# Raw weights one pair ahead, stores and reloads some steps behind their work, and reloads from ACT's queue, in two units of half products

## The chip, the cores and the metric

The kernel runs on one core of a Trainium2 chip. The engines of a core work side by side and wait for each other through semaphores: TensorE (PE in the profile), VectorE (DVE), ScalarE (ACT) and GpSimd (POOL) compute; each of them, and SyncE (SP), has a queue of its own that it works off in order. A transfer is issued from one of these queues: an instruction `sy.dma_start` stands in SP's queue, `ac.dma_start` in ACT's. It may wait there for its data or its buffer, and what stands behind it waits too. The metric is the device time of one execution in microseconds (us); lower is better.

## The reference

What is computed is one step of a layer of a streaming encoder: from the residual stream `x` (1,152 rows: 1,024 of a prompt and 8 x 16 of running streams; width 1,024) an input projection, two token mixers side by side (a state-space branch of width 2,048 and an attention branch of width 1,024), and then, cut to what the change touches:

```python
y = layer_norm(DN_ALPHA * x
               + (sigmoid(g_m) * (y_m @ w_br_m) + sigmoid(g_a) * (y_a @ w_br_a)) @ w_out)
```

`y_m` is 1,152 x 2,048, `y_a` 1,152 x 1,024, and each branch matrix projects to 1,024 columns. All of it is float32. The kernel holds every factor as two parts, `hi` (rounded) and `lo` (the rest), and makes a product of three matmuls: hi by hi, lo by hi, hi by lo.

## The kernel before

Up to about 1667 us of the profile the kernel computes the input projection, both mixers and the first half of `y_a @ w_br_a` (the quarter A0). The change touches what comes after, in four stages that PE works through in this order.

**Unit 0** (1667 to 1795 us) and **unit 1** (1850 to 1950 us) each compute one half of `y_m @ w_br_m` by half products in the manner of Winograd and Strassen: sums of blocks of rows (S1 to S4, D1, D2 and the plain blocks A11, A12, A22) by blocks of weights and their sums. Unit 0 takes rows 4 to 11 of the sixteen 128-row tiles of `y_m`, unit 1 the other eight. A unit (`unit`) has 4 pairs `p` of output columns; a pair has 8 pieces of weights, the plain blocks B11, B21, B12, B22 and the sums T1, T2, T4, T3, and takes 11 products. A product (`product`) is 12 matmuls of 128x128 by 128x384: three each over four steps k. After a pair's product its result is added into `acc` (DVE, L1485 and L1491) or copied there (ACT, L1483).

A piece is made three pieces ahead of its products by `prepare`. It has a tile `pc` in a ring of four (the tags `wh` and `wl`, two each): the sum of raw weights (L1423; on POOL in the first pair, else on DVE), the cast to the hi part on ACT (L1457), the lo part on POOL (L1458). The raw weights are `wu` (B11 and B21, one tile, loaded at L1411) and `wv` (B12 and B22, L1416); `load_pair` asks SP for the next pair's as soon as `prepare` has used this pair's. In the profile `u01d` is the fourth part of a name: unit 0, pair 1, accumulator d1 or d2; `u02m` is one of the m's of pair 2.

The sums T of unit 1 are made early, during unit 0, by the generator `sums_of_weights`: raw weights `we` to the tags `yr` (a ring of four) by SP at L1432, then for each of the four T's a sum on DVE (L1423), a cast on ACT (L1439), a lo part on DVE (L1440) into a tile `te`, and a store to `t_d` in memory by SP (L1441). Unit 1's `prepare` then only loads such a piece back (`pc<-t_d`, SP, L1454). The generator is worked off by `flow.tick()`, called twice in a product: `yield 3` lets three ticks pass before the next part is written into the queues. The order in which the units' instructions stand in each queue is the order in which this code writes them (`manual_schedule`); outside the units a planner with a cost model sets it.

After the sums, the same generator (`rows_c01`) loads the second half of the rows of `y_a` (`yr1`, L1587, and `yc1`, L1588) and makes them hi and lo (`part`, L1596 and L1597) for **quarter A1** (1795 to 1850 us, tile `dq`): the second half of `y_a @ w_br_a`, 288 matmuls, whose weights are `wr92` and the next (`fetch` L214, cast `wh` L226, lo part `wl` L227 on POOL). At the end of unit 0 (piece B22 of its last pair) stand `rows_c2` (the last third of those rows) and `first_rows(1)`, which loads the first two row tiles of unit 1 (`send`, L1338 and L1341) and scales them on DVE (`scaled`, L1345). The rest of unit 1's rows is loaded and summed during A1 by `load_sums` (hi parts L1329, lo parts L1330).

In unit 1 `seconds` fetches both halves of `y_a @ w_br_a` (`pa`, `pb`; L1640 and L1641) and the gate (L1642), adds them and multiplies (DVE, L1644 and L1646); `final` and `finish` load the other branch's gate (`gm`, L1654), multiply (DVE, L1662) and add (POOL, L1663). In this unit one product of each pair is copied by ACT to a tile `sh` (L1520).

**The out projection** (1950 to 2057 us, tile `out`) multiplies the merged rows U (`uhi` and `ulo`, made by `parts_of_u` on ACT L1689 and DVE L1690) with `w_out` (L1777 to L1779). The last third of the columns of `acc` is merged during it by `late` (L1676 to L1679, from tiles `lt`). A block of 128 rows that is done is normalized on DVE (L1807 to L1815) and stored.

Of the kernel before, what the change touches and what calls it, by code (L numbers as in the profile page):

```python
# [149 lines left out]
def trunk_step(ctx: ExitStack, tc: tile.TileContext, I, O):  # L150
# [1196 lines left out]
    def first_rows(v):  # L1347

        kts = ROWS[v]
        rb = [None]  # L1350
        pair_ = [send(kts[0], rb, *(() if v else (lazy["f0"], "gs"))), send(kts[1], rb)]
        for i in range(2):
            scaled(kts[i], pair_[i], rb)
        return pair_

    def load_sums(v, pair_=None):
# [5 lines left out]
        rb = [None]  # L1362
        pair_ = pair_ or first_rows(v)
        for i in range(4):
            y0, y1 = pair_
            if i:
                scaled(kts[2 * i], y0, rb)
                scaled(kts[2 * i + 1], y1, rb)
# [57 lines left out]
    def sums_of_weights():  # L1426

        early = {}
        for p in range(4, 8):
# [4 lines left out]
            if p == 4:  # L1434
                yield 4
            for i, n in enumerate(SUMS):
                x = sum_of(early, p, n, ve)
# [3 lines left out]
                sy.dma_start(t_d[4 * (p - 4) + i], o[:].bitcast(F32))  # L1441
                yield 3

    pieces = []

    def prepare():
# [6 lines left out]
        if p >= 4 and name in SUMS:  # L1453
            sy.dma_start(t[:].bitcast(F32), t_d[4 * (p - 4) + SUMS.index(name)])  # L1454
# [5 lines left out]
        if p % 4 < 3:  # L1460
            if name == ("T4" if p < 4 else "B21"):
                load_pair(p + 1, 0)
            if name == ("T3" if p < 4 else "B22"):
                load_pair(p + 1, 1)
# [112 lines left out]
    A1, ys = [], []  # L1577

    def rows_c01():
# [4 lines left out]
        for i in range(4):  # L1584
            y = mp.tile([P, T], F32, tag="yr", name=f"yr1{i}", bufs=4)[:, 0:2 * CW]
            ys.append(mp.tile([P, CW], F32, tag=("gt", "s4")[i % 2], name=f"yc1{i}", bufs=2)[:])
            sy.dma_start(y, ya_d[4 + i][:, 0:2 * CW])  # L1587
            sy.dma_start(ys[i], ya_d[4 + i][:, ch(2)])  # L1588
            yield 3
            for c in range(2):  # L1590
                part(c, i, y[:, ch(c)])
            yield 3
# [6 lines left out]
    def rows_c2():  # L1599

        A1.append(tuple(ap.tile([P, 4, CW], F32R, tag=f"a{x}2", name=f"ya1{x}2") for x in ("hi", "lo")))
        for i in range(4):
            part(2, i, ys[i])

    def steps_0(p, piece):

        if p == 3 and piece == "B22":
            flow.drain()
            rows_c2()
            lazy["rows"] = first_rows(1)  # L1610
# [23 lines left out]
    def seconds(*ps):  # L1634

        for j in (j for p in ps for j in (2 * p, 2 * p + 1)):
# [8 lines left out]
            yield 2  # L1645
            ve.scalar_tensor_tensor(g, t, 1.0, g, ALU.add, ALU.mult)  # L1646
            yield 1
# [24 lines left out]
    def late(j):  # L1672
# [3 lines left out]
        ve.tensor_tensor(x0, x0, x1, ALU.add)  # L1676
# [31 lines left out]
    def steps_1(p, piece):  # L1708
# [9 lines left out]
        if at == 5 and 0 < p < 3:  # L1718
# [192 lines left out]
```

## Time and profile before

| | us |
|---|---|
| median of 3 runs (lowest, highest) | 2062.91 (2058.42, 2064.49) |
| the profiled execution, its own time | 2066.38 |
| its span in the trace | 2064.6 |
| unit 0: 1667.0 to 1795.0 | 128.0 |
| quarter A1: 1795.0 to 1849.7 | 54.7 |
| unit 1: 1849.7 to 1950.3 | 100.6 |
| out projection: 1950.3 to 2057.3 | 107.0 |
| tail | 7.3 |

Over the whole span PE is busy 2021.1 us (98%), DVE 1355.0 (66%), ACT 951.5 (46%) and POOL 541.5 (26%). A row of the profile names a line, an engine, an operation and the tiles (out<-in), with start and duration or a count and a mean; in square brackets stands how long the engine was idle before it, and what ended that. `SPq` is SP's queue: a duration there is the time that its instructions held the queue, waiting included. A row of waits reads: who waited, for whom; us in total, times, longest us. The clock (PEclk) is the TensorE clock that was granted, as a share of full speed. A busy PE is not always PE at its own pace: the stages differ in the time that the same matmul takes.

### The profile page before, as it was taken

What the parts mean: (1) busy time and instruction counts of PE and PEld (TensorE: products, weight loads), DVE (VectorE), ACT (ScalarE), POOL (GpSimd) and SP (SyncE); (2) the same over time, 40 slices, a digit from 0 to 9 for tenths busy, and PEclk for the clock granted to TensorE, in tenths of its full rate; (3) what the DMA queues carried; (4) which work ended last, traced back from release to release, by engine and by line L of the source; (5) the groups of instructions that cost most, each with busy time, mean ns of one, the idle gap of its engine ahead of it and who ended that gap; (6) DMA issues with size and microseconds to landing.
All of it is one profiled execution on the core that took longest, in us unless ns stands there. A gap on an engine that the chain in (4) does not pass through costs nothing.

```text
span 2064.6 us, 36468 instructions
## 1 busy us (share of the span) xinstructions
PE 2021.1 (98%) x14199; PEld 1867.5 (90%) x14199; DVE 1355.0 (66%) x2237; ACT 951.5 (46%) x2059; POOL 541.5 (26%) x716
## 2 busy tenths in 40 slices
PE   9999999999999999999999999999999997899898
PEld 7899999999999999999888898898888987899886
DVE  4145666676766766633778778778677765566677
ACT  5124556456555555543555555544544543351310
POOL 0012535354544445331100100100010032313410
PEclk9999999999999999999999999999999998999998
DMA  7423232333233242425556666656657854477753
GB/s 220 162 65 99 72 125 84 123 95 123 90 117 120 78 148 67 140 95 180 174 190 214 201 184 214 194 188 206 192 181 227 281 183 163 174 239 279 263 181 107
DMA packets 139180, 332.37 MB, mean 161 GB/s; under 512 B 20360, under 2 KB 80256, under 8 KB 128768
## 3 DMA queue, kind: packets, MB, share of 16 engines
q1 hardware_dynamic: 121424, 238.75, 35.6%
q10 hardware_dynamic: 17584, 91.30, 12.9%
q8 instruction: 111, 1.82, 0.4%
q14 instruction: 61, 0.50, 0.1%
HBM read 255.66 MB, written 74.33 MB: 160 GB/s over the span
## 4 chain that ended last, share of the span: by engine, by line
PE 76%; DVE 9%; DMA 6%; issue 3%; POOL 3%; ACT 2%; SPq 0%; ACTq 0%; DVEq 0%; POOLq 0%
PE d L247 17%; PE d L249 16%; PE d L248 16%; PE s L953 3%; PE o L1028 2%; PE y L738 2%; PE v L337 2%; PE v L336 2%; PE v L335 2%; PE so L1103 1%; PE dS L679 1%; POOL pc L1458 1%; PE y L742 1%; PE ss L1081 1%; PE dq L249 1%
## 5 line engine op out<-in xcount | busy, mean ns | idle before, releaser
L247 PE MATMUL d<-xh,wh 128*128 128x384 f32 x2112 | 736.4, 349 | 0.0
L249 PE MATMUL d<-xh,wl 128*128 128x384 f32 x2112 | 708.3, 335 | 0.0
L248 PE MATMUL d<-xl,wh 128*128 128x384 f32 x2112 | 707.2, 335 | 0.0
L247 PEld LDWEIGHTS d<-xh,wh 128*128 128x128 f32 x2112 | 396.7, 188 | 19.4 <-issue 8.7
L248 PEld LDWEIGHTS d<-xl,wh 128*128 128x128 f32 x2112 | 397.2, 188 | 0.8
L249 PEld LDWEIGHTS d<-xh,wl 128*128 128x128 f32 x2112 | 396.5, 188 | 0.0
L227 POOL TENSOR_TENSOR wl<-wr,wh 128x1024 fp32r<-128x1024 f32 x37 | 89.9, 2429 | 180.2 <-ACT wh L226 168.2
L958 ACT ACTIVATE st<-s,ckt 128x256 f32<-128x256 f32 (+1 forms) x320 | 115.5, 469 | 16.5 <-PE s L953 14.2
L1018 ACT ACTIVATE st<-st 128x1024 f32<-128x1024 f32 x80 | 83.2, 1062 | 46.6 <-DVE st L1013 43.6
L962 POOL TENSOR_TENSOR st<-st,mask_bf 128x256 f32<-128x256 f32 x64 | 51.3, 822 | 192.4 <-ACT st L958 192.2
L707 ACT ACTIVATE m<-ce,nacum 128x128 f32<-128x128 f32 x288 | 96.9, 392 | 5.7 <-PE y L738 5.7
L230 DVE SCALAR_TENSOR_TENSOR wl<-wr,wh 128x1024 fp32r<-128x1024 f32 x50 | 62.1, 1243 | 34.9 <-ACT wh L229 34.8
L634 POOL TENSOR_TENSOR wx<-xdt,wdt 128x256 f32<-128x256 f32 x72 | 54.1, 753 | 85.2 <-DVE xdt L632 85.2
L1458 POOL TENSOR_TENSOR pc<-wu,pc 128x512 fp32r<-128x512 f32 x28 | 37.5, 1348 | 140.2 <-ACT pc L1457 140.2
L226 ACT CAST wh<-wr 128x1024 fp32r<-128x1024 f32 x48 | 50.3, 1049 | 51.0 <-PE d L248 44.6
L1028 PE MATMUL o<-st,vt 128*64 128x256 f32 (+1 forms) x640 | 69.4, 363 | 0.6
L1028 PEld LDWEIGHTS o<-st,vt 128*64 128x64 f32 x640 | 42.9, 136 | 27.3 <-ACT st L1018 4.0
L853 ACT ACTIVATE gate<-d,bcol 128x384 f32<-128x384 f32 x48 | 27.8, 578 | 72.2 <-PE d L249 47.1
L229 ACT ACTIVATE wh<-wr 128x1024 fp32r<-128x1024 f32 x50 | 52.7, 1054 | 14.3 <-PE d L248 10.7
L1039 DVE TENSOR_TENSOR st<-st 128x1024 f32<-128x1024 f32 (+1 forms) x40 | 57.4, 1436 | 0.8
L687 POOL TENSOR_TENSOR S<-S,ea 128x256 f32<-128x256 f32 x56 | 37.8, 675 | 75.9 <-DVE S L688 64.6
L336 PE MATMUL v<-vl,xh 128*128 128x512 f32 x144 | 56.4, 391 | 0.4 <-DVE vl L329 0.4
(929 smaller groups left out, 4372.1 us busy)
## 6 DMA issues: line engine op xcount, KB each, us to landing
wr<-in_wt SPq DMA_DIRECT2D x88, 512.0 KB
kc<-in_cache_k ACTq DMA_DIRECT2D x32, 1024.0 KB
vc<-in_cache_v ACTq DMA_DIRECT2D x32, 1024.0 KB
ce<-ac_d SPq DMA_DIRECT2D x96, 192.0 KB
sb<-cs_d ACTq DMA_DIRECT2D x16, 576.0 KB
yr<-ym_d SPq DMA_DIRECT2D x16, 576.0 KB
gate_d<-gate SPq DMA_DIRECT2D x45, 192.0 KB
s<-in_state_ssm SPq DMA_DIRECT2D x8, 1024.0 KB
```

Source lines behind the costliest of these rows:

```text
L227: lazy.get("sub", po).tensor_tensor(lo[:, :cols], raw[:, :cols], hi[:, :cols].bitcast(F32), ALU.subtract)
L230: ve.scalar_tensor_tensor(lo[:, :cols], raw[:, :cols], scale, hi[:, :cols].bitcast(F32), ALU.mult, ALU.subtract)
L247: te.matmul(out, wh, xh, start=(k == 0), stop=False)
L248: te.matmul(out, wh, xl, start=False, stop=False)
L249: te.matmul(out, wl, xh, start=False, stop=(k == n - 1))
L336: te.matmul(d, xh, wl, start=False, stop=False)
L707: ac.activation(m[:, j, :], ce[:, j * P:(j + 1) * P], AF.Abs, bias=nacum[:, b, h:h + 1])
L953: te.matmul(ps2[:, e, 256 * x + q0:256 * x + 256], kk[hr, ks], qq[hr, qs], start=(at == 0), stop=(at == 2))
L958: ac.activation(S[j][:, e, kb, q0:], ps2[:, e, 256 * x + q0:256 * x + 256], AF.Identity, bias=ckt[:, kb, 2 * hp + e:2 * hp + e + 1])
L1018: ac.activation(w, w, AF.Exp, scale=-1.0)
L1028: te.matmul(o[64 * e:64 * e + 64, 256 * at + q0:256 * at + 256], vt[:, kb, 64 * e:64 * e + 64], S[j][:, e, kb, q0:256], start=(kb == 0), s ...
L1458: po.tensor_tensor(t[:, 512:1024], out, t[:, 0:512].bitcast(F32), ALU.subtract)
```

## The change

The change moves work and adds none to PE. `sums_of_weights` loads the raw weights of the next pair after the first sum of the pair before, and issues each store to `t_d` one step later, ahead of the next sum. The rows `yr1` and `yc1` are loaded inside it (`load_second`) and no longer after it. `load_pair` is called some pieces later than before (`coming`: one piece in unit 0, two and three in unit 1). The reloads `pc<-t_d` stand in ACT's queue. `first_rows(1)` only sends, and one product earlier; the scaling stands at the start of `load_sums`. `seconds` runs once over all eight j at an even pace of ten ticks. In `late` the first add is on POOL; the late rows and the last `parts_of_u` come at other places of the out projection; `split_wo(3)` and `load_wo(6)` come before `finish(2)`, and `rows_of_wo` begins 0, 2, 3, 1.

```diff
--- before.py
+++ after.py
@@ -1348,10 +1348,7 @@
 
         kts = ROWS[v]
         rb = [None]
-        pair_ = [send(kts[0], rb, *(() if v else (lazy["f0"], "gs"))), send(kts[1], rb)]
-        for i in range(2):
-            scaled(kts[i], pair_[i], rb)
-        return pair_
+        return [send(kts[0], rb, *(() if v else (lazy["f0"], "gs"))), send(kts[1], rb)], rb
 
     def load_sums(v, pair_=None):
 
@@ -1359,13 +1356,11 @@
         slot.update({"A11": (Xb[0], 0), "A12": (Xb[0], 4), "A22": (Xb[1], 0), "S1": (Xb[1], 4),
                      "D1": (Xb[2], 0), "D2": (Xb[2], 4)})
         kts = ROWS[v]
-        rb = [None]
-        pair_ = pair_ or first_rows(v)
+        pair_, rb = pair_ or first_rows(v)
         for i in range(4):
             y0, y1 = pair_
-            if i:
-                scaled(kts[2 * i], y0, rb)
-                scaled(kts[2 * i + 1], y1, rb)
+            scaled(kts[2 * i], y0, rb)
+            scaled(kts[2 * i + 1], y1, rb)
             if i < 3:
                 pair_ = [send(kts[2 * i + 2], rb), send(kts[2 * i + 3], rb)]
             for name, y, c in (("D1", y0, c2), ("A11", y0, c0), ("D2", y1, c2), ("A12", y1, c0), ("A22", y1, c1)):
@@ -1425,23 +1420,52 @@
 
     def sums_of_weights():
 
-        early = {}
-        for p in range(4, 8):
+        early, stores = {}, []
+
+        def load(p):
             for j, names in enumerate((("B11", "B21"), ("B12", "B22"))):
                 t = mp.tile([P, 1024], F32, tag="yr", name=f"we{p}_{j}", bufs=4)
                 sy.dma_start(t[:], weights_of(p, j))
                 early[p, names[0]], early[p, names[1]] = t[:, 0:512], t[:, 512:1024]
-            if p == 4:
-                yield 4
+
+        def store():
+            for fn in stores:
+                fn()
+            stores.clear()
+
+        load(4)
+        yield 4
+        for p in range(4, 8):
             for i, n in enumerate(SUMS):
+                store()
+                if i == 1:
+                    if p < 7:
+                        load(p + 1)
+                    else:
+                        load_second(0)
+                        load_second(1)
                 x = sum_of(early, p, n, ve)
                 o = ap.tile([P, 1024], F32R, tag=("ahi0", "alo0", "ahi1", "alo1")[i], name=f"te{p}_{i}")
                 ac.copy(o[:, 0:512], x)
                 ve.tensor_tensor(o[:, 512:1024], x, o[:, 0:512].bitcast(F32), ALU.subtract)
-                sy.dma_start(t_d[4 * (p - 4) + i], o[:].bitcast(F32))
+                stores.append(lambda o=o, i=i, p=p: sy.dma_start(t_d[4 * (p - 4) + i], o[:].bitcast(F32)))
                 yield 3
-
-    pieces = []
+        store()
+        load_second(2)
+        load_second(3)
+        yield 4
+
+    rows2 = []
+
+    def load_second(i):
+
+        y = mp.tile([P, T], F32, tag="yr", name=f"yr1{i}", bufs=4)[:, 0:2 * CW]
+        yc = mp.tile([P, CW], F32, tag=("gt", "s4")[i % 2], name=f"yc1{i}", bufs=2)[:]
+        sy.dma_start(y, ya_d[4 + i][:, 0:2 * CW])
+        sy.dma_start(yc, ya_d[4 + i][:, ch(2)])
+        rows2.append((y, yc))
+
+    pieces, coming = [], []
 
     def prepare():
 
@@ -1451,17 +1475,18 @@
         if p >= 4 and name in SUMS:
-            sy.dma_start(t[:].bitcast(F32), t_d[4 * (p - 4) + SUMS.index(name)])
+            ac.dma_start(t[:].bitcast(F32), t_d[4 * (p - 4) + SUMS.index(name)])
         else:
             out = sum_of(raw, p, name, ve if p else po) if name in SUMS else raw[p, name]
             ac.copy(t[:, 0:512], out)
             po.tensor_tensor(t[:, 512:1024], out, t[:, 0:512].bitcast(F32), ALU.subtract)
         pieces.append(t)
         if p % 4 < 3:
-            if name == ("T4" if p < 4 else "B21"):
-                load_pair(p + 1, 0)
-            if name == ("T3" if p < 4 else "B22"):
-                load_pair(p + 1, 1)
+            for which, last, gap in ((0, "T4", 1), (1, "T3", 1)) if p < 4 else ((0, "B21", 2), (1, "B22", 3)):
+                if name == last:
+                    coming.append((n + gap, p + 1, which))
+        while coming and coming[0][0] <= n:
+            load_pair(*coming.pop(0)[1:])
 
     def product(d, n, name, first, last):
 
@@ -1574,7 +1599,7 @@
-    A1, ys = [], []
+    A1 = []
 
     def rows_c01():
 
@@ -1582,14 +1607,9 @@
         for c in range(2):
             A1.append(tuple(ap.tile([P, 4, CW], F32R, tag=f"a{x}{c}", name=f"ya1{x}{c}") for x in ("hi", "lo")))
         for i in range(4):
-            y = mp.tile([P, T], F32, tag="yr", name=f"yr1{i}", bufs=4)[:, 0:2 * CW]
-            ys.append(mp.tile([P, CW], F32, tag=("gt", "s4")[i % 2], name=f"yc1{i}", bufs=2)[:])
-            sy.dma_start(y, ya_d[4 + i][:, 0:2 * CW])
-            sy.dma_start(ys[i], ya_d[4 + i][:, ch(2)])
-            yield 3
             for c in range(2):
-                part(c, i, y[:, ch(c)])
-            yield 3
+                part(c, i, rows2[i][0][:, ch(c)])
+                yield 2
 
     def part(c, i, y):
         h, l = A1[c][0][:, i, :], A1[c][1][:, i, :]
@@ -1600,14 +1620,15 @@
 
         A1.append(tuple(ap.tile([P, 4, CW], F32R, tag=f"a{x}2", name=f"ya1{x}2") for x in ("hi", "lo")))
         for i in range(4):
-            part(2, i, ys[i])
+            part(2, i, rows2[i][1])
 
     def steps_0(p, piece):
 
+        if p == 3 and piece == "B12":
+            flow.drain()
+            lazy["rows"] = first_rows(1)
         if p == 3 and piece == "B22":
-            flow.drain()
             rows_c2()
-            lazy["rows"] = first_rows(1)
 
@@ -1631,9 +1652,9 @@
 
     G, U, wraw, pending, wo = {}, {}, {}, [], {}
 
-    def seconds(*ps):
-
-        for j in (j for p in ps for j in (2 * p, 2 * p + 1)):
+    def seconds():
+
+        for j in range(8):
             G[j] = mp.tile([P, T], F32, tag="yr", name=f"pa{j}", bufs=4)
             xt = ap.tile([P, 4 * CW], F32, tag="ahi0", name=f"pb{j}")
             g, x, t = G[j][:, 0:2 * CW], xt[:, 0:2 * CW], xt[:, 2 * CW:]
@@ -1642,9 +1663,9 @@
             sy.dma_start(t, gate_d[8 + j][:, 0:2 * CW])
             yield 5
             ve.tensor_tensor(g, g, x, ALU.add)
-            yield 2
+            yield 1
             ve.scalar_tensor_tensor(g, t, 1.0, g, ALU.add, ALU.mult)
-            yield 1
+            yield 4
 
     def final(*jcs):
 
@@ -1673,7 +1694,7 @@
 
         x0, x1, ta, tm = (pending.pop(0) for _ in range(4))
         a = acc[:, j, ch(2)]
-        ve.tensor_tensor(x0, x0, x1, ALU.add)
+        po.tensor_tensor(x0, x0, x1, ALU.add)
         ve.scalar_tensor_tensor(x0, ta, 1.0, x0, ALU.add, ALU.mult)
         ve.scalar_tensor_tensor(a, tm, 1.0, a, ALU.add, ALU.mult)
         po.tensor_tensor(a, a, x0, ALU.add)
@@ -1715,8 +1736,6 @@
             if at < 2:
                 final((b - 2, at))
             finish(1)
-        if at == 5 and 0 < p < 3:
-            flow.start(seconds(p + 1))
         if p == 0 and at == 4:
             load_wo(2)
         if p == 1 and at == 4:
@@ -1739,21 +1758,21 @@
     with tc.manual_schedule():
         sums_last(1)
         todo.pop(0)
-        flow.start(seconds(0, 1))
+        flow.start(seconds())
         unit(1, steps_1)
         flow.drain()
     sums_stack.close()
     raw_stack.close()
     op = ma_stack.enter_context(tc.tile_pool(name="op", bufs=1, reuse_waits="tile"))
     wo[0] = ready.pop(0)
-    finish(2)
+    split_wo(3)
+    load_wo(6)
     split()
     wo[1] = ready.pop(0)
-    split_wo(3)
-    load_wo(6)
+    finish(2)
     parts_of_u(0, (6, 7))
     load_late(0)
-    rows_of_wo = (0, 2, 1, 3, 4, 5, 6, 7)
+    rows_of_wo = (0, 2, 3, 1, 4, 5, 6, 7)
...
@@ -1786,14 +1805,14 @@
                     split_wo(k + 4)
                 if k == 2:
                     load_wo(7)
-                if k % 2:
-                    late(k // 2)
+                if k > 2:
+                    late(k - 3)
             parts_of_u(1, range(8))
         for j in range(3):
-            if c == 1 and j < 2:
-                late(4 + 2 * j)
-                late(5 + 2 * j)
-            if c == 1 and j == 2:
+            if c == 1 and j == 0:
+                for i in (5, 6, 7):
+                    late(i)
+            if c == 1 and j == 1:
                 parts_of_u(2, range(8))
...
```

What this does to the queues shows at three places. First SP's queue in unit 0, from the raw weights of pair 4 on (`we4`; `te4_0` is its first T). Before:

```order
L1432 DMA we4_0_18288<-in_wbr 128x1024
L1432 DMA we4_1_18290<-in_wbr 128x1024
L1441 DMA t_d_80<-te4_0_18326 128x1024
L1441 DMA t_d_80<-te4_1_18351 128x1024
L1411 DMA wu1_18377<-in_wbr 128x1024
L1441 DMA t_d_80<-te4_2_18386 128x1024
L1441 DMA t_d_80<-te4_3_18411 128x1024
L1416 DMA wv1_0_18420<-in_wbr 128x512
L1416 DMA wv1_1_18422<-in_wbr 128x512
L1432 DMA we5_0_18449<-in_wbr 128x1024
L1432 DMA we5_1_18451<-in_wbr 128x1024
L1441 DMA t_d_80<-te5_0_18454 128x1024
```

and now:

```order
L1428 DMA we4_0_18288<-in_wbr 128x1024
L1428 DMA we4_1_18290<-in_wbr 128x1024
L1451 DMA t_d_80<-te4_0_18326 128x1024
L1428 DMA we5_0_18350<-in_wbr 128x1024
L1428 DMA we5_1_18352<-in_wbr 128x1024
L1451 DMA t_d_80<-te4_1_18355 128x1024
L1451 DMA t_d_80<-te4_2_18388 128x1024
L1406 DMA wu1_18421<-in_wbr 128x1024
L1411 DMA wv1_0_18441<-in_wbr 128x512
L1411 DMA wv1_1_18443<-in_wbr 128x512
L1451 DMA t_d_80<-te4_3_18413 128x1024
L1451 DMA t_d_80<-te5_0_18454 128x1024
```

The loads `we5` moved from behind four stores and `wu1`, `wv1` to behind the first store; the last store of a pair moved behind `wu1` and `wv1`.

Second ACT's queue at the end of unit 0: `pc31` is the unit's last piece, `ya1hi2` and `wh92` are what quarter A1 needs, `ym1h` are parts of unit 1's rows. Before:

```order
L1457 CAST pc31_19086<-wv3_0_18877 128x512
L1483 COPY acc_17605<-u03d2_19106 128x384
L1596 CAST ya1hi2_19146<-yc10_18839 128x384
L1596 CAST ya1hi2_19146<-yc11_18906 128x384
L1596 CAST ya1hi2_19146<-yc12_18961 128x384
L1596 CAST ya1hi2_19146<-yc13_19021 128x384
L226 CAST wh92_19164<-wr92_19104 128x1024
L1329 CAST ym1h2_19203<-yr10_19156 128x384
L1329 CAST ym1h0_19199<-yr10_19156 128x384
L1329 CAST ym1h2_19203<-yr11_19160 128x384
L1329 CAST ym1h0_19199<-yr11_19160 128x384
L1329 CAST ym1h1_19201<-yr11_19160 128x384
```

and now:

```order
L1481 CAST pc31_19086<-wv3_0_18904 128x512
L1329 CAST ym1h0_19197<-yr10_19119 128x384
L1329 CAST ym1h0_19197<-yr11_19123 128x384
L1329 CAST ym1h1_19199<-yr11_19123 128x384
L1508 COPY acc_17605<-u03d2_19106 128x384
L1329 CAST ym1h2_19201<-yr10_19119 128x384
L1329 CAST ym1h2_19201<-yr11_19123 128x384
L1329 CAST ym1h1_19199<-yr11_19123 128x384
L1616 CAST ya1hi2_19152<-yc10_18741 128x384
L1616 CAST ya1hi2_19152<-yc11_18745 128x384
L1616 CAST ya1hi2_19152<-yc12_18843 128x384
L1616 CAST ya1hi2_19152<-yc13_18847 128x384
L226 CAST wh92_19162<-wr92_19104 128x1024
```

Six casts of `ym1h` stand ahead of the four of `ya1hi2` and of `wh92`; before they stood behind.

Third ACT's queue in the first pair of unit 1 (`sh0` is that pair's shared copy, `pc36` to `pc39` its last four pieces). Before:

```order
L1520 COPY sh0_19764<-u10m1_19750 128x384
L1457 CAST pc37_19797<-wv4_0_19714 128x512
L1457 CAST pc38_19820<-wv4_1_19716 128x512
L1457 CAST pc40_19861<-wu5_19614 128x512
L1457 CAST pc41_19878<-wu5_19614 128x512
L1520 COPY sh1_19973<-u11m1_19954 128x384
```

and now:

```order
L1478 DMA pc35_19728<-t_d_80 128x1024
L1545 COPY sh0_19764<-u10m1_19750 128x384
L1478 DMA pc36_19766<-t_d_80 128x1024
L1481 CAST pc37_19797<-wv4_0_19712 128x512
L1481 CAST pc38_19815<-wv4_1_19714 128x512
L1478 DMA pc39_19838<-t_d_80 128x1024
L1481 CAST pc40_19856<-wu5_19730 128x512
L1481 CAST pc41_19873<-wu5_19730 128x512
L1478 DMA pc42_19910<-t_d_80 128x1024
L1478 DMA pc43_19935<-t_d_80 128x1024
L1545 COPY sh1_19967<-u11m1_19952 128x384
```

The reloads stand between the copies and casts; `sh0` stands ahead of `pc36`, and `sh1` behind `pc43`.

## The prediction, made before the result was known

> **What bounds the kernel now.** The change touches only what runs after 1667 us, so I read that stretch first by stage (busy time of each engine in a window; after the window's bounds stands its length, PEclk is the granted TensorE clock as a share of full speed, and after it come the DMA share and GB/s). The rows are unit 0, quarter A1, unit 1 and the out projection.
>
> ```profile
> core 0: us, PE busy (x) PEld busy (x) DVE busy (x) ACT busy (x) POOL busy (x), PEclk, DMA share, GB/s
> 1667.00:1795.00 128.00, 107.36 (x530) 101.46 (x528) 65.96 (x100) 44.47 (x91) 46.38 (x34) 0.88 0.48 174
> 1795.00:1849.70 54.70, 52.01 (x290) 51.67 (x290) 41.86 (x59) 29.92 (x61) 13.49 (x6) 0.97 0.64 207
> 1849.70:1950.30 100.60, 94.55 (x530) 93.09 (x528) 60.96 (x90) 18.04 (x33) 37.01 (x28) 0.98 0.78 271
> 1950.30:2057.30 107.00, 102.59 (x481) 85.20 (x480) 78.11 (x141) 16.90 (x32) 17.29 (x10) 0.97 0.49 165
> ```
>
> TensorE (PE) is the bound in all four stages, but not at its own pace. That pace is in the records of the quarter before, where nothing waits:
>
> ```profile
> L247 PE MATMUL dq<-ya0h,wh x96: 334/334/334, 1617.1 to 1666.5; 128*128 128x384 f32 x96
> L249 PE MATMUL dq<-ya0h,wl x96: 334/334/334, 1617.5 to 1666.9; 128*128 128x384 f32 x96
> ```
>
> Three such lines make 288 matmuls between 1617.1 and 1666.9, 49.8 us or 0.173 us each. A unit has 528 of the same shape, so 91.6 us. Unit 0 therefore loses 128.0 - 91.6 = 36.4 us, A1 (288 matmuls) 54.7 - 49.9 = 4.8, unit 1 100.6 - 91.6 = 9.0. The waits of PE from 1667 us on say what for (total, times, longest, us):
>
> ```profile
> PE u01d L1471 <- ACT pc L1457: 8.8, 2, 6.1
> PE u02m L1471 <- ACT pc L1457: 6.1, 2, 3.1
> PE u12m L1471 <- DMA pc<-t_d: 3.8, 2, 3.2
> PE dq L249 <- POOL wl L227: 2.0, 1, 2.0
> PE out L1777 <- ACT uhi L1689: 1.7, 1, 1.7
> PE u11m L1471 <- DMA pc<-t_d: 1.6, 1, 1.6
> PE out L1779 <- DVE ulo L1690: 1.1, 1, 1.1
> PE u00m L1471 <- ACT pc L1457: 1.0, 1, 1.0
> PE u00m L1473 <- POOL pc L1458: 0.7, 1, 0.7
> PE dq L247 <- ACT wh L226: 0.7, 1, 0.7
> ```
>
> In unit 0 four stalls of PE, 14.9 us, end with the cast of a piece. The cast is not slow; it is late. Inside that unit's window VectorE (DVE) and SP's queue wait thus:
>
> ```profile
> DVE we L1423 <- DMA we<-in_wbr: 23.0, 3, 8.3
> DVE te L1440 <- ACT te L1439: 14.6, 16, 2.4
> SPq L1441 <- DVE te L1440: 59.7, 13, 9.3
> ```
>
> SP issues in order, and the store of one `te` tile makes it wait for DVE. So everything behind a store is late: the next pair's `we` loads, and `wu`. These rows of SP's timeline show it (start, duration; the four stores hold the queue from 1701 to 1715, and `wu` comes after):
>
> ```profile
> 1691.27 0.90 SPq L1432 DMA_DIRECT2D we<-in_wbr  x2
> 1701.08 12.18 SPq L1441 DMA_DIRECT2D t_d<-te  x4
> 1715.59 0.33 SPq L1411 DMA_DIRECT2D wu<-in_wbr  x1
> ```
>
> A `we` load asked for at 1691.7 lands at 1698.85; the DVE stands before its sum for 8.33 us, and behind that sum in DVE's queue stands what PE needs. First the chain of waits, then the timeline:
>
> ```profile
> 1691.74 7.11 DMA we<-in_wbr
> ```
>
> ```profile
> 1698.94 0.69 DVE L1423 TENSOR_TENSOR we<-we,we 128x512 f32<-128x512 f32 x1 [8.33 <-DMA we<-in_wbr]
> 1700.89 0.69 PE L1471 MATMUL u01d<-ym0h,pc 128*128 128x384 f32 x1 [2.74 <-ACT pc L1457]
> 1703.06 0.52 PE L1472 MATMUL u01d<-ym0l,pc 128*128 128x384 f32 x1
> 1703.38 0.52 PE L1473 MATMUL u01d<-ym0h,pc 128*128 128x384 f32 x1
> ```
>
> The last two rows are the second price: after the gap the matmuls start 0.32 us apart, not 0.173, each 0.147 us late. Unit 0's idle time on PE is 128.0 - 107.36 = 20.6 us; the other 15.8 of its 36.4 are about 107 matmuls at that half pace, which is why the window's clock reads 0.88. A stall costs its gap and some 20 matmuls (3 us) behind it.
>
> **The change, part by part.** Durations (count, total, mean ns, idle before), from unit 0:
>
> ```profile
> L1458 POOL TENSOR_TENSOR pc<-wu,pc 128x512 fp32r<-128x512 f32 x18 | 23.5, 1310 | 48.5 <-ACT pc L1457 48.5
> L1440 DVE TENSOR_TENSOR te<-we,te 128x512 fp32r<-128x512 f32 x16 | 15.5, 968 | 14.6 <-ACT te L1439 14.6
> L1439 ACT CAST te<-we 128x512 fp32r<-128x512 f32 x16 | 9.9, 619 | 38.3 <-DVE we L1423 36.4 <-issue 2.0
> L1423 DVE TENSOR_TENSOR we<-we,we 128x512 f32<-128x512 f32 x8 | 8.2, 1019 | 23.0 <-DMA we<-in_wbr 23.0
> ```
>
> *Raw weights one pair ahead, stores one step behind (unit 0).* No instruction is removed. A `we` pair is now asked for behind the first store of the pair before, some three quarters of a pair (11 products of 12 matmuls, 22.9 us) ahead of its first sum, against a load of 7.11 us. That covers DVE's three load waits, 23.0 us, and with them the three largest stalls on PE. A store issued one step later finds its lo part done, so SP's 59.7 us of waiting shrink and `wu`, `wv` follow in time; each of those goes behind at most three stores, all ready. What is late next is DVE's own order. A step is sum 1.02, cast 0.62 on ACT, lo 0.97, so 2.6 us in line; in the second pair two such steps (5.2 us) stand ahead of the sum for T4, and that piece needs cast 0.62 and POOL 1.31 behind it. In the first pair the T sums are on POOL in both kernels, and nothing there changes. I leave to the four pairs 3.4 us (its two short gaps on `u00m`, 1.7, and some 11 slow matmuls, 1.6), 4.5 (between nothing and 5.2 + 3), 2.5 and 1: 11.4 together. Gain 36.4 - 11.4 = 25.0. Bounds: the three load stalls alone (11.8 us of gaps and 3 us each behind, so 20.8, less 3 for a new T4 stall) give 18; everything but 5 us gives 31. If the early loads collided with others, the cover of 17 us less 7.11 would have to go first.
>
> [...]
>
> *First rows of unit 1 scaled before the last rows of A1 (end of unit 0).* The row loads move by one product. But on ACT six casts of `ym1` now stand ahead of the four `ya1hi` casts and of `wh92`, with which A1 begins. DVE, ACT and POOL of before, each from its timeline:
>
> ```profile
> 1793.48 1.96 DVE L1597 TENSOR_TENSOR ya1lo<-yc,ya1hi 128x384 fp32r<-128x384 f32 x4
> 1795.37 4.84 DVE L1345 SCALAR_TENSOR_TENSOR yr<-yr,mcol,rsb 128x1152 f32<-128x1152 f32 x2
> ```
>
> ```profile
> 1792.94 1.75 ACT L1596 CAST ya1hi<-yc 128x384 fp32r<-128x384 f32 x4 [1.60 <-PE u03m L1473]
> 1794.60 1.04 ACT L226 CAST wh<-wr 128x1024 fp32r<-128x1024 f32 x1
> ```
>
> ```profile
> 1795.77 3.21 POOL L227 TENSOR_TENSOR wl<-wr,wh 128x1024 fp32r<-128x1024 f32 x1 [4.65 <-ACT wh L226]
> ```
>
> Before, `wh92` was done at 1795.64, 0.6 us after unit 0's end, for which PE waited 0.7, and then 2.0 for `wl`. Now six casts (2.6 us at the 0.44 of a `ya1hi` cast) and the two scalings that they wait for come first. In SP's timeline the loads are asked for 10 us ahead of the unit's end:
>
> ```profile
> 1784.98 0.43 SPq L1338 DMA_DIRECT2D yr<-ym_d  x1
> ```
>
> So the scalings are mostly under unit 0; I put `wh92` 2.4 us after the unit's end, so 1.8 more idle and some 8 slow matmuls more: 3 us lost. Bounds: 0 (all six done under the last product) and 7 (the whole 4.84 and the casts after it).
>
> *Reloads from ACT's queue, loads with a gap, `seconds` at an even pace (unit 1).* The stalls were SP's order too: `pc<-t_d` stood behind `pb`, whose buffer waited for DVE. From the chain of waits there:
>
> ```profile
> 1897.68 5.99 DMA pb<-pa_d
> ...
> 1908.54 4.87 DMA pc<-t_d
> ```
>
> From the buffer's release to its use four to five products of 2.08 us (12 x 0.173) pass, 8.3 to 10.4 us; the reload takes 4.87. On ACT the instruction waits for the same product that frees the buffer; ahead of it can stand one `sh` copy, which is ready about 1 us after that. So 2 to 4 us are spare. The sixteen issues of 0.4 us each on ACT are nothing: it is busy 18.04 of 100.6 us. The three DMA stalls (5.4 us) and their slow matmuls (about 3) go, and I leave 3 of the 9.0: gain 6, from 2 to 8.
>
> *Late rows (out projection).* The eight first adds leave DVE for POOL, which is busy 17.29 of 107.0; all `late` parts are done sooner, and the last third of U (the out projection's input) is made one column group earlier. The two stalls there (`uhi` 1.7, `ulo` 1.1) and about 2.7 us of slow matmuls behind them can go, 5.5; what is earlier makes other DVE work later in a stage where DVE is busy 78.11 of 107.0, so gain 4, from 1.5 to 5.5. `split_wo(3)` ahead of `finish(2)`: the start waits for the last product's add as before, nothing. The tail is unchanged.
>
> The sum: -25 + 3 - 6 - 4 = -32. The profiled execution took 2066.38 (span 2064.6), so 2034.4. It lies 3.5 above the median of the runs, 2062.91; against that the same 32 give **2031**.
>
> **The rivals.**
>
> *DVE's queue takes the place of the loads.* The T4 stall that I give to one pair comes in three, each as large as a before one: a 3 us gap with 3 us behind. 18 instead of the 8 left for these pairs, 10 more, and a slower A1 (2): 2043. For it speaks the 14.6 us that DVE stands for its own cast round trip, inside the queue that also carries the piece sums; against it, that DVE's 65.96 us fill only 64% of the 103 us that unit 0 would take.
>
> *Nearly all goes.* Unit 0 keeps only its first pair's 3.4 (-33), A1 0, unit 1 -8, out -5: 46 us, 2017. The 17 us of cover speak for it; the DVE order against.
>
> *Slower: reloads that share the DMA engines.* In unit 1 the reloads no longer queue behind SP's loads but run beside them, at a stage whose share is 0.78 and which would run faster still. If a reload beside another 512 KB load takes twice 4.87 us, 9.7, it passes the 8 us budget by about 1.7, plus 3 us of slow matmuls: 4.7 a piece. It decides from 8 us of transfer on; with twelve of the sixteen hit, 56 us, so 2031 + 6 + 56 = 2093, and with nine 2079. Against it: unit 1 moves 271 GB/s, 27.3 MB, which in 95 us are 287 GB/s, and the loads on SP are now spread evenly. [...]
>
> *The change doesn't do what it says:* stores one step behind still wait for lo parts, and SP's queue stays the bound with `wu` behind three stores. Then unit 0 gains only about 5, the rest stands: 2063 - 5 + 3 - 6 - 4, 2051.
>
> **How the numbers follow.** Forecast 0.50, DVE's queue 0.22, nearly all 0.13, slower 0.08, not as said 0.07. The forecast's own bounds, all best or all worst, are -44.5 and -14.5 (2018 to 2048); the range takes in the rivals on both sides but the slower one: 2015 to 2052. A measurement of this kernel tells about 0.3% (6.2 us) from no change. Faster, below 2056.7: the first three and half of the last, 0.88; within 0.3%: 0.06; slower: 0.06.
>
> **What would show it.** Unit 0 at about 103 us with DVE's waits on `we` gone and SP's on `te` small; if it stays above 115 with waits of PE on `pc` casts behind DVE, the first rival holds. A1 at 57 to 58, its first matmul 2 to 3 us after unit 0's last; a shorter A1 refutes my third step. Unit 1 at 94 to 95, no wait on `pc<-t_d`; more of these waits than three would be the reloads' rival. Out at 103, no waits for `uhi` and `ulo` in its middle. The prediction is wrong altogether if unit 0 is not the stage that changes most.

## The result, and the profile after

| | before | after |
|---|---|---|
| median, us (lowest to highest) | 2062.86 (2058.42 to 2064.49) | 2030.66 (2027.91 to 2032.09) |
| profiled execution, own time / span | 2066.38 / 2064.6 | 2031.07 / 2029.3 |
| unit 0 | 128.0 | 99.7 |
| quarter A1 | 54.7 | 55.9 |
| unit 1 | 100.6 | 96.7 |
| out projection | 107.0 | 102.9 |

The ratio is 0.9846, 95% interval 0.9827 to 0.9864: faster by 32 us. The four stages of the kernel after, in the view by windows (columns as before):

```profile
1666.80:1766.50 99.70, 95.52 (x529) 92.84 (x527) 74.02 (x101) 44.21 (x91) 47.77 (x34) 0.98 0.65 229
1766.50:1822.40 55.90, 53.05 (x288) 52.54 (x289) 39.34 (x56) 28.83 (x59) 12.72 (x6) 0.94 0.56 187
1822.40:1919.10 96.70, 93.69 (x530) 93.39 (x529) 59.75 (x89) 17.93 (x32) 37.59 (x28) 0.98 0.80 285
1919.10:2022.00 102.90, 100.64 (x482) 84.63 (x480) 74.30 (x133) 17.44 (x33) 26.54 (x19) 0.98 0.52 173
```

28.3 of the 35.3 us between the two spans come from unit 0. (The profiled execution before was 3.5 us above its median, so the spans differ by more than the medians do.) Unit 0's four stalls of 14.9 us are gone; PE's longest waits after 1667 us are now these:

```profile
PE u12m L1496 <- DMA pc<-t_d: 3.0, 1, 3.0
PE dq L247 <- ACT wh L226: 2.6, 1, 2.6
PE out L1797 <- DVE wl L230: 2.2, 1, 2.2
PE u01m L1496 <- ACT pc L1481: 1.3, 1, 1.3
PE u02m L1498 <- POOL pc L1482: 0.9, 2, 0.7
PE u01m L1498 <- POOL pc L1482: 0.7, 1, 0.7
PE u00m L1498 <- POOL pc L1482: 0.7, 1, 0.7
```

In unit 0 DVE has no wait for a `we` load any more (it was 23.0 us). The raw weights of pair 6 are asked for at 1692.84 and first used at 1704.84, with the DVE busy up to that moment. SP's queue and then DVE's, from the timeline:

```profile
1692.84 1.25 SPq L1428 DMA_DIRECT2D we<-in_wbr  x2
1695.84 8.83 SPq L1451 DMA_DIRECT2D t_d<-te  x3
```

```profile
1703.63 0.69 DVE L1450 TENSOR_TENSOR te<-we,te 128x512 fp32r<-128x512 f32 x1 [0.69 <-ACT te L1449]
1704.24 0.69 DVE L1418 TENSOR_TENSOR wu<-wu 128x512 f32<-128x512 f32 x1
1704.84 0.68 DVE L1418 TENSOR_TENSOR we<-we,we 128x512 f32<-128x512 f32 x1
```

The second row of DVE's is the sum for T4 in the second pair; it comes behind two steps of `te`, and PE waits for its piece, the one longer stall that unit 0 has left. It isn't new: the kernel before had it at the same product (1.2 us for the cast, 0.7 for the lo part). The rows of the changed kernel:

```profile
1705.69 0.44 PE L1496 MATMUL u01m<-ym0h,pc 128*128 128x384 f32 x1 [1.28 <-ACT pc L1481]
1707.05 0.48 PE L1498 MATMUL u01m<-ym0h,pc 128*128 128x384 f32 x1 [0.74 <-POOL pc L1482]
1707.64 0.52 PE L1497 MATMUL u01m<-ym0l,pc 128*128 128x384 f32 x1
```

### The profile page after: what moved, and what is told of

The parts are those of the page before. It is cut to its first block, busy times and chain, and to the rows that moved or that the text cites. A ratio compares the mean times of both kernels' runs of the same rounds, so it can differ in the third digit from the quotient of the medians.

```text
span 2029.3 us, 36477 instructions
## 1 busy us (share of the span) xinstructions
PE 2006.7 (99%) x14199; PEld 1859.9 (92%) x14199; DVE 1356.7 (67%) x2229; ACT 951.6 (47%) x2059; POOL 551.6 (27%) x724
## 5 line engine op out<-in xcount | busy, mean ns | idle before, releaser
L335 PE MATMUL v<-vh,xh 128*128 128x512 f32 x144 | 56.9, 395 | 0.8 <-ACT vh L328 0.8
```

The source lines that it names most:

```text
L335: te.matmul(d, xh, wh, start=(k == 0), stop=False)
```

## The experiments

All stage times are read as above, from the first matmul of a stage to that of the next (a unit to its last). Ratios are against the kernel before, with 95% intervals.

### Which half of the SP edit carries unit 0

The kernel before with the loads moved alone:

```diff
+        load(4)
+        yield 4
+        for p in range(4, 8):
             for i, n in enumerate(SUMS):
+                if i == 1 and p < 7:
+                    load(p + 1)
```

> The kernel before, with one part of the change alone: the raw weights of the next pair are loaded behind the first sum of the pair before; stores are issued at once as before, the rows of A1, the reloads and the rest as before. My theory (the loads' lateness is the cost): DVE's waits on the raw weights (23.0 us in unit 0) go, and with them three stalls of PE (11.8 us of gaps and the slow matmuls behind); unit 0 falls from 128 to about 108, the time to about 2043. Rival (the stores that wait for DVE hold SP's queue, and the piece loads behind them are as late as the raw weights were): unit 0 stays above 118, the time above 2052.

Measured: 2038.88 us, ratio 0.9890 (0.9872 to 0.9908). Unit 0 of this kernel, and SP's wait for DVE in it:

```profile
1665.70:1770.50 104.80, 97.29 (x529) 94.23 (x527) 66.48 (x98) 43.52 (x88) 47.52 (x34) 0.97 0.59 210
```

```profile
SPq L1446 <- DVE te L1445: 37.6, 12, 9.4
```

The theory holds: 23 of unit 0's 28 us come from the earlier loads alone; the median is 24 us lower. The kernel before with the stores one step behind alone:

```diff
             for i, n in enumerate(SUMS):
+                store()
                 x = sum_of(early, p, n, ve)
...
+                stores.append(lambda o=o, i=i, p=p: sy.dma_start(t_d[4 * (p - 4) + i], o[:].bitcast(F32)))
```

> The kernel before, with the other part alone: each store is issued one step behind its lo part; the raw weights are still asked for at the start of their own pair. My theory: the loads are asked for some 2 us sooner at best and still land 5 us after DVE wants them; unit 0 about 121, the time about 2056. Rival (the stores were the cause): SP's wait on DVE goes, unit 0 falls to about 105 and the time to about 2040.

Measured: 2064.37 us, ratio 1.0008 (0.9995 to 1.0022), no change. Unit 0, and DVE's waits for the loads there:

```profile
1664.10:1794.00 129.90, 104.17 (x529) 99.30 (x527) 64.87 (x98) 43.63 (x89) 46.37 (x34) 0.91 0.48 171
```

```profile
DVE we L1423 <- DMA we<-in_wbr: 24.9, 3, 9.3
```

DVE waits for the same loads as long as before. The rival falls, and so does my expectation of a small gain. SP's wait for DVE doesn't go either: 45.1 us are left of 59.7.

The last 5 us of unit 0 (104.8 to 99.7) come with the stores behind, the rows `yr1` and `yc1` loaded sooner and the later `load_pair`. No run tried these three apart, but the traces show where the 5 us lie. The kernel with the loads alone has one long stall left, on `u02m` in the third pair. ACT waits there for the rows `yr1`, DVE waits for ACT, and the sum for T3's piece stands behind that in DVE's queue. ACT's queue, DVE's and PE's wait:

```profile
1737.83 0.93 ACT L1601 CAST ya1hi<-yr 128x384 fp32r<-128x384 f32 x2 [6.32 <-DMA yr<-ya_d]
```

```profile
1738.37 1.03 DVE L1602 TENSOR_TENSOR ya1lo<-yr,ya1hi 128x384 fp32r<-128x384 f32 x2 [5.58 <-ACT ya1hi L1601]
...
1740.71 0.68 DVE L1423 TENSOR_TENSOR wv<-wv,wv 128x512 f32<-128x512 f32 x1
```

```profile
PE u02m L1476 <- ACT pc L1462: 3.0, 1, 3.0
```

The kernel before has the same row, and its fourth stall, 3.1 us, stands behind it:

```profile
1761.89 0.93 ACT L1596 CAST ya1hi<-yr 128x384 fp32r<-128x384 f32 x2 [6.47 <-DMA yr<-ya_d]
```

So of the four stalls before, the raw weights made three, and the rows `yr1` the fourth. In the kernel with the loads alone the first of these rows are asked for at 1731.80, in the changed kernel at 1722.97, and that stall is gone. With the slow matmuls behind it (PE is busy for 97.29 us with the same 529 matmuls, for 95.52 in the changed kernel), it makes up the 5 us; that the earlier rows alone would bring them is read from the traces and not tried.

### Unit 1: the queue of the reloads and the pace of the loads

The changed kernel with `sy.dma_start` for `pc<-t_d`:

> The changed kernel, with the reloads of unit 1 in SP's queue again. My theory: they stand behind loads whose buffers wait for DVE; unit 1 goes from 96.7 to about 100, the time to about 2034. Rival 1 (the even pace of the other loads is what freed unit 1): unit 1 and the time stay, 2031. Rival 2 (ACT's queue is itself the cause of the one stall left, 3.0 us, since the reload stood there behind a copy that waited for DVE): that stall goes, unit 1 about 93, the time about 2027.

Measured: 2024.67 us, ratio 0.9823 (0.9803 to 0.9842); unit 1:

```profile
1821.90:1915.40 93.50, 92.20 (x529) 91.69 (x529) 60.11 (x89) 17.70 (x32) 36.59 (x28) 1.00 0.81 292
```

My theory, that SP's queue was the reloads' trouble, fell, and the second rival came out: the stall of 3.0 us is gone. A smaller one, 1.3 us in the unit's first pair, has come, behind a reload that took 8.44 us. The chain of waits of the changed kernel shows the place: a 384 KB load of the gate takes 8.86 us, DVE's sum waits for it, the add into `acc` waits behind that in DVE's queue, ACT's copy `sh` for the add, and the reload stands behind the copy in ACT's queue:

```profile
1867.60 8.86 DMA pb<-gate_d
...
1876.54 0.96 DVE pa L1667
...
1878.00 0.04 ACT sh L1545
...
1878.36 5.57 DMA pc<-t_d
```

Then the other edit of this stage: the loads of `seconds` in bursts again, with the reloads on ACT and, in a second kernel, on SP:

```diff
-        flow.start(seconds())
+        flow.start(seconds(0, 1))
...
+        if at == 5 and 0 < p < 3:
+            flow.start(seconds(p + 1))
```

> The changed kernel, with the loads of both halves of y_a's product (seconds) in bursts as before, pairs 0 and 1 at once and 2 and 3 when their time comes. The run with the reloads on SP made unit 1 faster (93.5 against 96.6 us), so the reloads' queue isn't what freed that stage. My theory now: the even pace is; with the bursts the loads stand before DVE early and long, ACT's copy waits for DVE, and the reload behind that copy is late. Unit 1 goes from 96.6 to about 101, the time to about 2035. Rival (the later piece loads, two and three pieces, freed it): unit 1 stays within 1 us of 96.6, the time at 2031.

> The changed kernel with the bursts of before and the reloads in SP's queue too, so that of unit 1's edits only the later piece loads are left. Theory (the pace decides, the queue matters only by what stands ahead in it): about as the kernel before, unit 1 near 100, the time about 2034. Rival (with bursts SP's queue is full, and only ACT's queue helps there): clearly slower than the run with bursts and ACT's queue, by 3 us or more. Second rival (later piece loads alone free it): unit 1 near 94, the time about 2025.

Measured: 2032.08 us, ratio 0.9859 (0.9830 to 0.9889), and 2030.41 us, 0.9841 (0.9815 to 0.9867). Unit 1 with bursts on ACT, and with bursts on SP:

```profile
1820.00:1919.40 99.40, 94.86 (x531) 93.29 (x529) 57.86 (x90) 18.45 (x33) 37.36 (x28) 0.98 0.77 277
```

```profile
1822.90:1920.70 97.80, 93.49 (x529) 91.56 (x528) 59.93 (x90) 18.08 (x33) 37.43 (x28) 1.00 0.78 283
```

So in this stage the even pace is worth 2.7 us with ACT (99.4 to 96.7) and 4.3 with SP (97.8 to 93.5); ACT's queue gains nothing in either row. How the bursts cost it is not quite as I said: with ACT's queue PE's longest wait is 2.1 us for a lo part on POOL (`u11d`), and the waits for reloads are 1.0 and 0.8; why that lo part was late is open. The totals don't tell either kernel from the changed one's 2030.66, and the stage itself varies: the same unit 1 as in the changed kernel took 94.6 and 94.3 us in the two kernels of the out projection below. Even so, apart from the kernel with three edits below, no profile with the even pace is above 96.7, and none with bursts below 97.8. The later piece loads alone, with bursts and SP as before, leave 97.8; unit 1 of the kernel before took 100.6 and 100.9 in two profiles, and 100.0 and 97.9 in the two one-part kernels above. Those loads are worth 3 us at most, and perhaps nothing.

### A1: the first rows of unit 1

The changed kernel with `first_rows` as before (sent and scaled behind `rows_c2`):

> The changed kernel, with the first rows of unit 1 sent and scaled where they were before (after the last rows of A1). My theory (those casts ahead of wh cost A1 its start): PE's wait for wh falls from 2.65 to about 0.7, that for wl comes back at up to 2.0, A1 goes from 55.9 to about 54.5, the time to about 2029. Rival (A1's start is bound by the weights' load or by POOL, whatever stands on ACT): A1 stays at 56, the time at 2031.

Measured: 2026.59 us, ratio 0.9834 (0.9816 to 0.9851). A1, and PE's two waits at its start:

```profile
1767.00:1822.80 55.80, 53.12 (x289) 52.73 (x289) 43.25 (x60) 30.02 (x61) 13.24 (x6) 0.94 0.58 198
```

```profile
PE dq L249 <- POOL wl L227: 2.0, 1, 2.0
...
PE dq L247 <- ACT wh L226: 0.7, 1, 0.7
```

The waits came as expected, but A1 is only 0.1 us shorter: 0.7 + 2.0 against 2.65 + 0.2. So the casts ahead of `wh` hardly explain why A1 takes longer than the 54.7 us of before. What differs is the clock: it is 0.94 in this row and in the changed kernel's, 0.97 before; 14 matmuls start 0.32 us apart there in the changed kernel, 10 before. The median is 4 us lower, which no row of A1 explains; in the profile it is unit 1, 94.0 us, where the stall on `u12m` is 1.6 us and not 3.0, and the clock is 1.00 and not 0.98. Why the stall is shorter is open.

In the changed kernel the chain into A1 runs through the scaling, as its chain of waits shows:

```profile
1760.88 1.42 DVE yr L1345
...
1766.39 1.75 ACT ya1hi L1616 x4
1768.13 0.96 ACT wh L226
...
1769.22 2.38 POOL wl L227
```

### The out projection

The changed kernel with the late rows as before, and then with the order of splits and rows as before too:

```diff
-        po.tensor_tensor(x0, x0, x1, ALU.add)
+        ve.tensor_tensor(x0, x0, x1, ALU.add)
...
-                if k > 2:
-                    late(k - 3)
+                if k % 2:
+                    late(k // 2)
```

> The changed kernel with the late rows as before: first add on DVE, their places and that of the last parts of U in the out projection as before. My theory: the stalls on uhi and ulo in the second column group come back, the out projection goes from 103.0 to about 106.5, the time to about 2034. Rival (the stage's gain came from what lies before it, since a kernel without this edit already had 102.9 there): the stage stays within 1 us, the time at 2031.

> The changed kernel with all of the out projection's edits undone: the late rows as before, the split of the output weights behind the last finish(2), and the order of rows 0, 2, 1, 3. Putting the late rows back alone changed nothing (103.2 against 103.0 us). Theory (the gain of that stage belongs to the order of the splits and rows): it goes to about 107, the time to 2034. Rival (it belongs to no edit there; the stage varies by some 4 us with what comes before it): it stays between 101 and 104, the time at 2031.

Measured: 2031.04 us, ratio 0.9847 (0.9817 to 0.9877), and 2030.06 us, 0.9844 (0.9830 to 0.9857). The stage, in this order:

```profile
1917.80:2021.00 103.20, 100.94 (x482) 84.59 (x480) 80.35 (x141) 17.34 (x33) 17.45 (x11) 0.98 0.50 172
```

```profile
1915.80:2020.20 104.40, 101.00 (x482) 84.57 (x480) 80.11 (x141) 17.36 (x33) 18.61 (x11) 0.98 0.49 170
```

Both theories fall; the second's rival, up to 104, is missed by 0.4. The late rows are worth 0.3 us, all edits of this stage 1.5, and the total shows neither. The stalls on `uhi` and `ulo` don't come back in either kernel, so it isn't these edits that took them away. Where, then, are the 4 us between 107.0 and 102.9? The kernel before, profiled once more:

> The kernel before, unchanged, once more with a profile. If the stages of the first profile are its own, unit 0 is 128, A1 54.6, unit 1 100.7 and the out projection 107.0 within 1 us each. Rival: unit 1 and the out projection move by 2 us or more between executions of one program, and the gains read from one pair of profiles there are not sizes of an edit.

Its time was 2060.39 us; unit 0 was 126.0, A1 54.6, unit 1 100.9, and the out projection

```profile
1947.20:2051.30 104.10, 99.91 (x481) 83.25 (x479) 78.11 (x141) 16.88 (x32) 17.28 (x10) 1.00 0.51 170
```

So 3 of the 4 us belong to the one execution of the first profile, and 2 of unit 0's 28 as well. Both profiles have the same two stalls in the second column group, 1.71 and 1.06 us in the first, 1.50 and 1.06 in the second; the granted clock after them differs. The first profile from the second stall on, then the second profile from within the first stall on:

```profile
2025.00:2030.00 5.00, 3.94 (x10) 2.98 (x10) 4.86 (x11) 0.29 (x1) 0.00 (x0) 0.52 0.42 125
```

```profile
2020.00:2025.00 5.00, 2.80 (x11) 2.02 (x12) 4.93 (x8) 0.51 (x1) 0.54 (x1) 1.00 0.28 105
2025.00:2030.00 5.00, 5.00 (x24) 4.14 (x23) 3.54 (x7) 0.29 (x1) 0.00 (x0) 1.00 0.80 266
```

### A version that beats both

Three edits on the changed kernel: reloads on SP; `rows_c2` behind the last product of unit 0 and the first part of `load_sums` written into unit 0's fixed order, so that `wh92` comes first on ACT; the last `finish(2)` and `parts_of_u` written into unit 1's fixed order, so that the first output weights' lo part stands ahead of them on DVE.

```diff
-        if p == 3 and piece == "B22":
+        if p == 3 and piece == "T3":
             rows_c2()
...
         unit(0, steps_0)
         flow.drain()
+        flow.start(load_sums(1, lazy["rows"]))
+        flow.step()
...
         unit(1, steps_1)
         flow.drain()
+        finish(2)
+        parts_of_u(0, (6, 7))
```

> The changed kernel with three edits: reloads on SP; unit 1's first sums written after the weights of A1, whose split is written ahead of the last rows of A1; the last finish(2) and parts of U written inside unit 1's fixed order, so that the lo part of the first output weights stands ahead of them on DVE. Theory: unit 1 about 93.5; PE's waits at A1's start (2.65 and 0.2, with 14 matmuls at half pace behind, 2 us) go, A1 about 51; the wait of 2.2 on wl goes with 1 us of slow matmuls, out about 100; together 11 us less, about 2020. Rival (the casts and sums that are now later cost as much where they are wanted: ya1 of the last column block, or the rows of unit 1): A1 stays at 55 or above and unit 1 begins with waits on ym1, the time no better than 2024.

Measured: 2023.66 us, ratio 0.9813 (0.9789 to 0.9837). A1, and from the chain of waits the third reload of unit 1:

```profile
1766.50:1816.30 49.80, 49.80 (x289) 49.80 (x288) 43.01 (x62) 27.82 (x59) 11.71 (x5) 1.00 0.65 229
```

```profile
1823.93 8.39 DMA pc<-t_d
```

A1 now runs at PE's own pace (288 matmuls in 49.8 us), and the out projection takes 100.3; but unit 1 goes to 99.3, since PE waits 3.1 us for that reload. A fourth edit starts `seconds` four ticks later (`yield 4` ahead of its loop):

> The kernel with three edits, and a fourth: the first loads of both halves of y_a's product (pa, pb, gate: 1.15 MB) are asked for four ticks (about 4 us) later. In the run with three edits, A1 ran at PE's own pace (49.8 us), but the third reload of unit 1 took 8.39 us, with 3.1 MB of loads asked for in the 6 us around it, and PE waited 3.1 us. Theory (the loads that start with the unit share the DMA engines with that reload): the wait goes, unit 1 falls from 99.3 to about 94.5, the time from 2023.7 to about 2019. Rival (the reload is late by its place in SP's queue or by the stores of A1): the wait of 3 us stays, the time at 2023.

Measured: **2020.00 us**, ratio 0.9793 (0.9778 to 0.9808). Unit 1:

```profile
1817.10:1911.20 94.10, 92.98 (x530) 91.67 (x529) 61.19 (x91) 18.45 (x34) 38.01 (x28) 1.00 0.83 300
```

No wait on `pc<-t_d` is left. But the edit did less, and something else, than I meant. Counted from the unit's first matmul, the first `pa` load goes out at 6.5 us and not at 6.1. It stands behind the third reload now and no longer ahead of it, and the reload goes out at 6.0 us, not at 7.6. SP's queue with three edits, and with four:

```profile
1822.36 0.37 SPq L1662 DMA_DIRECT2D pa<-pa_d  x1
...
1823.93 0.39 SPq L1478 DMA_DIRECT2D pc<-t_d  x1
```

```profile
1823.09 0.37 SPq L1478 DMA_DIRECT2D pc<-t_d  x1
1823.56 0.44 SPq L1663 DMA_DIRECT2D pa<-pa_d  x1
```

By the trace's semaphores that reload now takes 6.8 us. So it lands 3.2 us earlier in the unit, 1.6 by its place in SP's queue and 1.6 by a shorter transfer, and this run doesn't part theory and rival. Last, this kernel with the reloads on ACT again:

> The fastest kernel so far (four edits, 2020.0 us), with the reloads in ACT's queue again, as the change has them. Theory (a reload on ACT stands behind the shared copy, which stands behind DVE's sums and the load of pb; in SP's queue it doesn't): one reload a pair late by up to 3 us, unit 1 from 94.1 to about 96.5, the time to about 2023. Rival (the queue is of no account once nothing ahead of it is late): unit 1 within 1 us of 94.1, the time within 1.5 us of 2020.

Measured: 2019.36 us, ratio 0.9806 (0.9788 to 0.9823). Unit 1:

```profile
1814.70:1908.80 94.10, 92.56 (x529) 91.62 (x528) 62.15 (x91) 18.58 (x34) 37.30 (x28) 1.00 0.84 305
```

The rival came out: as far as these two kernels tell, the queue is of no account once nothing that stands ahead in it is late.

## Why the prediction was right, point by point

The time was predicted at 2031 and measured at 2030.66. The mechanism of the largest term was right; three smaller terms had errors of size or of cause that cancelled, so that a hit to 0.3 us is luck.

*Unit 0: 25.0 predicted, 28.3 measured* (26.3 against the second profile of before). The late loads were the cause, and T4's piece in the second pair is late, as said, though not next: that stall, 1.2 and 0.7 us, stood in the kernel before and in every other run. I had no term for the rows `yr1`; the fourth stall, which I took for gone with the rest, went with their earlier loads. I left 11.4 us; 8.1 are left (99.7 - 91.6). The first pair keeps one gap of 0.7 and no slow matmuls, 1.2 us (3.4 said), the second gaps of 0.5, 1.28 and 0.74 and ten slow ones, 4.9 (4.5 said), the third 0.9 of gaps, 1.6 (2.5), the last none (1). Two steps failed in detail. The loads are not 17 us ahead but 12.0: the sums follow each other by the generator's ticks, not once in a pair. And the stores one step behind still find DVE late: SP's wait for it is 36.4 us, not small. It does not matter, since the loads no longer stand behind it. Nor were `wu` and `wv` late by the stores alone: SP also waited for their buffers, which POOL frees, 24.7 us before and 15.0 now.

*The half pace.* I put 107 slow matmuls into unit 0's 15.8 us beside the gaps. The records show 58 of them there, 8.5 us; the rest, 7 us, lies at the first matmuls around each gap, which start up to 0.49 us apart. Nor do the records show the 20 slow matmuls, 3 us, that I put behind each stall: behind the four long ones there are 15, 8, 10 and 14, which lose 1.2 to 2.2 us, and 11 behind the gaps on `u00m`. The sum, 36.4, didn't depend on it.

*A1: 3 us lost predicted, 1.2 measured.* `wh92` was 2.65 us late where I said 2.4. The step that failed is that I left the wait for `wl` (2.0) in place behind it: the two lie in one chain, and when `wh` waits longer the wait for `wl` shrinks to 0.2. The matmuls at half pace behind them were 10 before and are 14 now. Undoing the edit gave back 0.1 us, so most of the 1.2 lies in that slow stretch and not in a wait for the casts.

*Unit 1: 6 predicted, 3.9 measured.* The cause was wrong. I gave the gain to ACT's queue; the runs give it to the even pace, with 3 us at most for the later piece loads, and the queue added the one stall that stayed. The size belongs to one pair of profiles: with 94.6 and 94.3 us, the same unit in two other kernels, the gain is 6. That a copy `sh` ahead of the reload is ready within about 1 us is the sentence that failed: it was late by the load of the gate, through DVE's queue.

*Out projection: 4 predicted, 4.1 measured, and not by its reason.* The edits there are worth 1.5 us at most; the other 2.6 to 2.9 were slow matmuls of one execution. At the stage's start, where I put nothing, PE's wait for `wl` grew from 1.6 to 2.2 us.

*The rivals.* DVE's queue did not take the loads' place: one stall, not three. The slower case, reloads beside other loads, was to decide from 8 us of transfer on. By the semaphores of its trace the changed kernel's sixteen reloads took 3.6 to 7.8 us, so none got there. In other runs single ones did: 8.44 us on SP with a wait of PE of 1.3, and 8.39 with three edits and a wait of 3.1. The kernel before had one of 8.9. The forecast's side of the line was right, by little.

## What to carry to other kernels

In an in-order queue that issues transfers, ask for what has a long way to come before anything that waits for an engine: moving the loads alone gave 23 us, moving the stores that wait gave none. Before giving a queue of its own to a transfer, look at what stands ahead of it there, and from where that is late; when nothing late stood ahead of it, both queues gave the same 94.1 us. Follow every stall to its own first cause: the four stalls of unit 0 looked alike and had two. Read a stage's gain of a few us from two profiles of the same program before crediting it to an edit.

## What the runs showed of the hardware

Gaps of like length do not always cost the same. In the out projection of the kernel before, 1.71 + 1.06 us of idle PE were followed by twelve matmuls that start 0.43 us apart, where the others start 0.23 apart; in another execution of the same program 1.50 + 1.06 us were followed by none. The stall at T4's piece, 1.0 to 1.5 us and then 0.7, is in all fourteen traces. Behind it ten matmuls start 0.32 us apart in the changed kernel (1.28 + 0.74), which lose 1.5 us together; in the kernel before (1.21 + 0.72) and in the one with the stores alone (0.97 + 0.73) none do.

The stall on `u12m` shows the same. In the changed kernel it takes 3.02 us, and ten matmuls start 0.32 us apart soon behind it:

```profile
1884.07 0.41 PE L1496 MATMUL u12m<-ym1h,pc 128*128 128x384 f32 x1 [3.02 <-DMA pc<-t_d]
1884.32 0.34 PE L1497 MATMUL u12m<-ym1l,pc 128*128 128x384 f32 x1
1884.49 0.34 PE L1498 MATMUL u12m<-ym1h,pc 128*128 128x384 f32 x1
1884.67 0.40 PE L1496 MATMUL u12m<-ym1h,pc 128*128 128x384 f32 x1
1884.86 0.52 PE L1497 MATMUL u12m<-ym1l,pc 128*128 128x384 f32 x1
```

With the late rows as before it takes 2.45 us, and none do:

```profile
1884.35 0.41 PE L1496 MATMUL u12m<-ym1h,pc 128*128 128x384 f32 x1 [2.45 <-DMA pc<-t_d]
1884.60 0.34 PE L1497 MATMUL u12m<-ym1l,pc 128*128 128x384 f32 x1
1884.78 0.34 PE L1498 MATMUL u12m<-ym1h,pc 128*128 128x384 f32 x1
1884.95 0.33 PE L1496 MATMUL u12m<-ym1h,pc 128*128 128x384 f32 x1
```

So the length of a stall alone does not tell: 2.45 us left the matmuls behind it at their pace, and the shorter gaps of 1.28 and 0.74 did not. What decides it, these runs don't show.
